# Down projections in block-product pairs, and one buffer for the sums of x and of h, in a decoder layer

## The chip, the cores and the metric

One core of a Trainium2 chip runs the whole layer in one launch. The time is device microseconds, the median of the runs of one kernel. The profile is one execution of the same program, taken by the hardware profiler; its span runs from the first to the last instruction of the program.

## What is computed

One decoder layer on x of 256 tokens by 2048 columns, float32, in four residual steps: a SwiGLU half-step, a mixer (attention beside gated linear attention), cross-attention into 256 memory tokens, and a second SwiGLU half-step. The change is in the half-steps:

```python
def swiglu(h, w_gate, w_up, w_down):
    return (jax.nn.silu(h @ w_gate) * (h @ w_up)) @ w_down

x = x + 0.5 * swiglu(rms_norm(x, ffn1_norm[l]), ffn1_w_gate[l], ffn1_w_up[l], ffn1_w_down[l])
...
x = x + 0.5 * swiglu(rms_norm(x, ffn2_norm[l]), ffn2_w_gate[l], ffn2_w_up[l], ffn2_w_down[l])
```

The gate and up weights are 2048 x 5632, the down weights 5632 x 2048.

## The kernel before

**Numbers and tiles.** Every float32 operand is split into a high and a low half (ScalarE casts the high one, L136; VectorE subtracts for the low one, L137), and a product of two operands is three matmuls: high by high, high by low, low by high. A weight block is 512 rows by 512 columns: 1 MiB, one DMA from SP (L132), one cast, one subtraction, and then for both halves of the tokens (128 each) 4 x 3 matmuls of 128x512. So a block costs TensorE 24 matmuls in plain form (`mm3`, L158 to L165).

**A half-step** (`ffn`, L345 to L397). The 5632 middle columns are 11 chunks of 512, taken in three parts: chunks 0 to 3, 4 to 7, and 8 to 10. For each chunk of a part the gate and the up projection are made, silu and the product give h, TensorE transposes it two steps later (`turn`, L349 to L357; the low half is made at L274, without high priority), and at the end of the part the down projection adds its share to x: for each of 4 output chunks, one block for each chunk of the part (L392 to L393), and an eviction to x by VectorE (L395). After the last part the first half-step starts the norm of each finished chunk (`norm_chunk`), the second one stores it.

**Seven block products.** From the second chunk on, gate and up of one chunk are made as a pair (`strassen`, L198 to L252). The left and right weights of the first two row groups and the two token halves form a 2 by 2 by 2 block product, done with seven products instead of eight. A product is 12 matmuls (`product`, L188 to L196). It wants sums of blocks: those of x are made once for each half-step (`sums_of`, L173 to L186, called at L390) and stay in the tiles sh and sl. Those of the weights are made on the way, two on VectorE (L212) and two by a DMA of POOL that adds into its target (L216). The results meet in four accumulators: c0l and x on the left, c0r and c1r on the right. The other two row groups are then added in plain form (L247 to L251). The last product, with the summed block ral, stands ahead of these groups at L245:

```python
        accumulate(ral, rbl)
        product(x, s_(2), parts(rar), False)
        ...
        product(c0r, s_(3), parts(rbr), False)
        product(x, of(b, 1), parts(ral), False)
        accs = ((c0l, x), (c0r, c1r))
```

**What sets the order.** A scheduler fixes the order of each engine's instructions ahead of the run: of those that are ready by its own account it takes the one of best priority. Weight loads, splits and sums are traced with a priority as if they stood 200 instructions earlier (`tc.high_priority(WPRI)`). On the chip each engine, and each engine's DMA queue, keeps that order. Buffers: six for raw weights, three pairs (FWB) for split weights, eight for h and for what `sums_of` needs on the way (tag "h"), one each for sh and sl.

Of the kernel before, what the change touches and what calls it, by code (L numbers as in the profile page):

```python
# [16 lines left out]
P = 128  # L17
S = 256
TT = S // P
D = 2048  # L20
NC = D // 512
# [6 lines left out]
WPRI = 200  # L28
# [17 lines left out]
PARTS = ((0, 1, 2, 3), (4, 5, 6, 7), (8, 9, 10))  # L46
# [3 lines left out]
def layer_kernel(ctx: ExitStack, tc: tile.TileContext, A: dict, out: bass.AP):  # L50
    nc = tc.nc
    V, SC, G, PE, SY = nc.vector, nc.scalar, nc.gpsimd, nc.tensor, nc.sync
# [1 line left out]
    con = ctx.enter_context(tc.tile_pool(name="con", bufs=1))  # L54
    wp = ctx.enter_context(tc.tile_pool(name="wp", bufs=3))
    sp = ctx.enter_context(tc.tile_pool(name="sp", bufs=SB))
    st = ctx.enter_context(tc.tile_pool(name="st", bufs=10))
    pa = ctx.enter_context(tc.tile_pool(name="pa", bufs=4, space=PSUM))
    pm = ctx.enter_context(tc.tile_pool(name="pm", bufs=4, space=PSUM))

# [13 lines left out]
    def FT(tag, bufs, shape, dt, name):  # L74
        return phase["pool"].tile(shape, dt, tag=tag, name=name, bufs=bufs)
# [94 lines left out]

    def sums_of(ga, gb, put):  # L173

        (ah, al), (bh, bl) = ga, gb
        fa, fb = (FT("h", 8, [P, 4, S], F32, n) for n in ("fa", "fb"))
        V.tensor_add(fa, ah.bitcast(F32), al.bitcast(F32))
        V.tensor_add(fb, bh.bitcast(F32), bl.bitcast(F32))
        t0, t1 = slice(0, P), slice(P, S)
        sa, sb = (FT("h", 8, [P, 2, 4, P], F32, n) for n in ("sa", "sb"))  # L180
        V.tensor_sub(sa[:, 0], fa[:, :, t1], fb[:, :, t1])
        V.tensor_sub(sa[:, 1], sa[:, 0], fa[:, :, t0])
        V.tensor_sub(sb[:, 0], fa[:, :, t0], fa[:, :, t1])
        V.tensor_add(sb[:, 1], fb[:, :, t0], sa[:, 1])
        for i, x in enumerate((sa, sb)):
            split(*put(i), x)  # L186

    def product(acc, lhs, w, start):  # L188

        wh, wl = w  # L190
        first = start
        for i, j, w in ((0, 0, wh), (1, 0, wh), (0, 1, wl)):
            for k in range(4):
                PE.matmul(acc, lhs(k)[i], w[:, k], start=first, stop=j == 1 and k == 3, skip_group_check=not start)  # L194
                first = False
        tick()  # L196

    def strassen(Wl, cl, Wr, cr, lhs, ab, sums, groups):  # L198

        a, b = ab  # L200
        ral, rar = load(Wl, cl, a), load(Wr, cr, a)
        rbr, rbl = load(Wr, cr, b), load(Wl, cl, b)

        def parts(src):
            with tc.high_priority(WPRI):
                wh, wl = (FT(x, FWB, [P, 4, 512], F32R, x) for x in ("wh", "wl"))
                split(wh, wl, src)
            return wh, wl

        def add(dst, x, y):  # L210
            with tc.high_priority(WPRI):
                V.tensor_add(dst, x, y)  # L212

        def accumulate(dst, x):
            with tc.high_priority(WPRI):
                G.dma_start(dst, x, accum_op=ALU.add)  # L216

        def of(g, t):
            return lambda k: lhs(4 * g + k, t)

        def s_(i):
            return lambda k: tuple(x[:, i, k] for x in sums)
# [12 lines left out]
        add(ral, ral, rbr)  # L235
        product(x, s_(1), parts(ral), False)
        with tc.high_priority(WPRI):
            V.tensor_sub(c0r, ys, x)
        product(c0l, of(b, 0), parts(rbl), False)
        accumulate(ral, rbl)  # L240
        product(x, s_(2), parts(rar), False)
        with tc.high_priority(WPRI):
            V.tensor_sub(c1r, ys, x)
        product(c0r, s_(3), parts(rbr), False)
        product(x, of(b, 1), parts(ral), False)  # L245
        accs = ((c0l, x), (c0r, c1r))
        for i, g in enumerate(groups):  # L247
            for acc, W, c in zip(accs, (Wl, Wr), (cl, cr)):
                for h, half in enumerate(wgroup(W, c, g)):
                    mm3(acc, lhs, half, False, i == len(groups) - 1 and h == 1, seeded=True)  # L250
                    tick()  # L251
        return accs  # L252

    def proj(W, c, lhs, groups, fine=None, last=False):

        n = W.shape[-1]
        acc = [pa.tile([P, n], F32, tag="acc", name="acc") for _ in range(TT)]
        groups = list(groups)
        for i, g in enumerate(groups):
            if fine and i:  # L260
                fine(4 * i)
            if last and i == len(groups) - 1:
                both = [w for half in wgroup(W, c, g) for w in half]
                for t in range(TT):
                    mm3(acc, lhs, both, i == 0, True, (t,))
                break
# [10 lines left out]
    xT = {}  # L277
# [67 lines left out]
    def ffn(pre, r, after, fine=None, last=False):  # L345
        wg, wu, wd = (A[f"{pre}_w_{n}"] for n in ("gate", "up", "down"))
        hT = {}

        def turn(f, hs):  # L349
            hi, lo = (FT("h", 8, [P, 4, S], F32R, n) for n in ("hTh", "hTl"))  # L350
            for t in range(TT):
                tp = PM([P, 4, P], "tp")
                for j in range(4):
                    PE.transpose(tp[:, j], hs[t][:, j * P:(j + 1) * P], ident)  # L354
                sl = slice(t * P, (t + 1) * P)
                split_from_psum(hi[:, :, sl], lo[:, :, sl], tp)
# [6 lines left out]
        sums = None  # L363
        for part in PARTS:
            for f in part:
                if sums is None:
                    gate = proj(wg, f, lhs_x, range(4), fine)
                    if callable(r):
                        r = r()
                else:  # L370
                    gate, upv = strassen(wg, f, wu, f, lhs_x, (0, 1), sums, (2, 3))
                sg = []
                with tc.high_priority(WPRI):
                    for t in range(TT):
                        s = W2([P, 512], "sg")
                        SC.activation(s, gate[t], AF.Silu, scale=r[:, t:t + 1])
                        sg.append(s)
                if sums is None:
# [8 lines left out]
                if sums is None:  # L387
                    sums = tuple(FT(n, 1, [P, 4, 4, P], F32R, n) for n in ("sh", "sl"))
                    with tc.high_priority(WPRI):
                        sums_of(xT[0], xT[1], lambda i: tuple(p[:, 2 * i:2 * i + 2] for p in sums))  # L390
            end = part is PARTS[-1]
            for c in range(NC):  # L392
                acc = proj(wd, c, lhs_h, part, last=last and end and c == NC - 1)  # L393
                for t in range(TT):
                    V.scalar_tensor_tensor(xs[c][:, t], acc[t], 0.5, xs[c][:, t], op0=ALU.mult, op1=ALU.add)  # L395
                if end:
                    after(c)  # L397


    def head_scale(acc, r, r2, t, scale_in, sign, name):  # L400
# [633 lines left out]
```

## Time and profile before

| | |
|---|---|
| median of 3 runs | 1975.95 us (1974.84 to 1976.38) |
| the profiled execution | 1974.94 us |
| its span | 1972.9 us |
| TensorE busy | 1942.4 us, 8760 matmuls |
| VectorE busy | 1276.1 us |
| ScalarE busy | 989.3 us |
| DMA | 416.14 MB, mean 211 GB/s |

The busy time of TensorE is modelled from matmuls that overlap, so it says that TensorE has work, not that it is at its peak. What a matmul costs is read from the distance between starts in a stretch in which it never waits. The first half-step runs from the start to about 740 us, the middle of the layer to about 1240 us, the second half-step to the end. In each half-step three stretches of down projection follow the parts. Names in the rows: acc, x and y are accumulators, xTh, hTh, sh and xTl, hTl, sl the high and low halves of x, of h and of the sums, wh and wl those of weights, raw a weight block as it was loaded.

### The profile page before, as it was taken

How to read it: one execution, taken by the hardware profiler on the slowest of the kernel's cores; microseconds unless marked ns; L12 is line 12 of the kernel's file. 1: busy time of each engine (PE TensorE's matmuls, PEld its weight loads, DVE VectorE, ACT ScalarE, POOL GpSimd, SP SyncE). 2: the span in 40 equal slices, each digit the busy share in tenths (PEclk: the TensorE clock that was granted, in tenths of full speed). 3: DMA queues.
4: the chain of work that ended last, by engine and by line, in shares of the span. 5: the costliest groups of instructions: out<-in, count | busy, mean ns of one | idle time of the engine just before them, and what ended most of it. 6: DMA issues, size and time to landing. Idle time of an engine off the chain costs nothing.

```text
span 1972.9 us, 21472 instructions
## 1 busy us (share of the span) xinstructions
PE 1942.4 (98%) x8760; PEld 1587.5 (80%) x8760; DVE 1276.1 (65%) x1027; ACT 989.3 (50%) x956; POOL 97.6 (5%) x101
## 2 busy tenths in 40 slices
PE   8999999999999999999999999899999999999999
PEld 7878887778877888778888889677788777887787
DVE  6776467774577655546785566677746777457763
ACT  5555345553355446444676445555534555335542
POOL 2000000000000000002220000000000000000000
PEclk9999999999999999999999999899999999999999
DMA  9677557775567725445466554566755777556771
GB/s 364 234 232 252 187 156 269 263 260 193 171 221 230 274 88 181 156 167 189 170 219 217 182 192 155 208 234 224 246 191 152 268 263 263 197 179 213 234 278 64
DMA packets 63294, 416.14 MB, mean 211 GB/s; under 512 B 7099, under 2 KB 8251, under 8 KB 14428
## 3 DMA queue, kind: packets, MB, share of 16 engines
q1 hardware_dynamic: 56284, 370.74, 49.7%
q0 software_dynamic: 5760, 41.95, 10.4%
q10 hardware_dynamic: 1152, 2.10, 0.3%
q8 instruction: 68, 1.11, 0.2%
q14 instruction: 30, 0.25, 0.0%
HBM read 370.72 MB, written 2.10 MB: 189 GB/s over the span
## 4 chain that ended last, share of the span: by engine, by line
PE 89%; DVE 6%; ACT 2%; issue 2%; DMA 1%; SPq 0%; POOL 0%; DVEq 0%; ACTq 0%
PE acc L164 22%; PE acc L165 22%; PE acc L163 22%; PE x L194 8%; DVE wl L137 5%; PE acc L194 4%; ACT wh L136 2%; PE y L194 2%; PE x L164 2%; PE x L165 2%; PE x L163 2%; PE tp L354 1%; DVE raw L212 1%; DMA xr<-in_xT_dram 1%; PE tp L314 0%
## 5 line engine op out<-in xcount | busy, mean ns | idle before, releaser
L137 DVE TENSOR_TENSOR wl<-raw,wh 128x2048 fp32r<-128x2048 f32 (+2 forms) x487 | 933.6, 1933 | 594.5 <-ACT wh L136 593.2
L136 ACT CAST wh<-raw 128x2048 fp32r<-128x2048 f32 (+2 forms) x487 | 777.3, 1615 | 705.0 <-PE acc L165 494.4
L164 PE MATMUL acc<-wl,xTh 128*128 128x512 f32 x1024 | 406.3, 397 | 13.7 <-DVE wl L137 13.4
L163 PE MATMUL acc<-wh,xTh 128*128 128x512 f32 x1024 | 405.9, 398 | 6.7 <-ACT wh L136 6.7
L165 PE MATMUL acc<-wh,xTl 128*128 128x512 f32 x1024 | 403.6, 394 | 0.0
L163 PE MATMUL acc<-wh,hTh 128*128 128x512 f32 x704 | 274.7, 390 | 0.0
L165 PE MATMUL acc<-wh,hTl 128*128 128x512 f32 x704 | 274.0, 389 | 0.0
L164 PE MATMUL acc<-wl,hTh 128*128 128x512 f32 x704 | 274.0, 389 | 0.0
L164 PEld LDWEIGHTS acc<-wl,xTh 128*128 128x128 f32 x1024 | 194.1, 190 | 65.3 <-DVE wl L137 24.1
L163 PEld LDWEIGHTS acc<-wh,xTh 128*128 128x128 f32 x1024 | 193.7, 190 | 50.5 <-ACT wh L136 7.6
L165 PEld LDWEIGHTS acc<-wh,xTl 128*128 128x128 f32 x1024 | 194.0, 189 | 42.3
L165 PEld LDWEIGHTS acc<-wh,hTl 128*128 128x128 f32 x704 | 132.2, 188 | 27.5
L163 PEld LDWEIGHTS acc<-wh,hTh 128*128 128x128 f32 x704 | 132.2, 188 | 27.3
L164 PEld LDWEIGHTS acc<-wl,hTh 128*128 128x128 f32 x704 | 132.2, 188 | 27.1
L216 POOL DMA_DIRECT2D raw<-raw x40 | 34.7, 867 | 1191.1 <-DVE raw L212 978.4
L212 DVE TENSOR_TENSOR raw<-raw 128x2048 f32<-128x2048 f32 x40 | 91.5, 2287 | 0.7
L163 PE MATMUL x<-wh,xTh 128*128 128x512 f32 x160 | 62.8, 392 | 0.0
L164 PE MATMUL x<-wl,xTh 128*128 128x512 f32 x160 | 62.6, 391 | 0.0
L165 PE MATMUL x<-wh,xTl 128*128 128x512 f32 x160 | 62.5, 391 | 0.0
L228 ACT COPY acc<-x 128x512 f32<-128x512 f32 x20 | 11.4, 571 | 97.9 <-PE x L194 97.9
L395 DVE SCALAR_TENSOR_TENSOR x<-acc,x 128x512 f32<-128x512 f32 x48 | 33.0, 688 | 31.7 <-PE acc L165 31.7
L163 PE MATMUL acc<-wh,mTh 128*128 128x512 f32 x128 | 50.2, 392 | 0.0
(302 smaller groups left out, 1966.0 us busy)
## 6 DMA issues: line engine op xcount, KB each, us to landing
raw<-in_ffn_w_up_dram SPq DMA_DIRECT2D x88, 1024.0 KB, 7.0
raw<-in_ffn_w_down_dram SPq DMA_DIRECT2D x88, 1024.0 KB, 5.1
raw<-in_ffn_w_gate_dram SPq DMA_DIRECT2D x85, 1024.0 KB, 7.6
raw<-in_w_in_dram SPq DMA_DIRECT2D x48, 1024.0 KB, 4.8
raw<-raw POOLq DMA_DIRECT2D x40, 1024.0 KB, 6.9
raw<-in_w_out_dram SPq DMA_DIRECT2D x16, 1024.0 KB, 4.8
raw<-in_xattn_w_k_dram SPq DMA_DIRECT2D x4, 1024.0 KB, 4.8
raw<-in_xattn_w_q_dram SPq DMA_DIRECT2D x4, 1024.0 KB, 4.7
```

Of the source, the lines that this page charges most:

```text
L136: SC.copy(wh, src)
L137: V.tensor_sub(wl, src, wh.bitcast(F32))
L163: PE.matmul(acc[t], lh, wh, start=first and i == 0, stop=False, skip_group_check=seeded)
L164: PE.matmul(acc[t], lh, wl, start=False, stop=False, skip_group_check=seeded)
L165: PE.matmul(acc[t], ll, wh, start=False, stop=last and i == len(half) - 1, skip_group_check=seeded)
L194: PE.matmul(acc, lhs(k)[i], w[:, k], start=first, stop=j == 1 and k == 3, skip_group_check=not start)
L212: V.tensor_add(dst, x, y)
L216: G.dma_start(dst, x, accum_op=ALU.add)
L228: SC.copy(c0l, x)
L354: PE.transpose(tp[:, j], hs[t][:, j * P:(j + 1) * P], ident)
L395: V.scalar_tensor_tensor(xs[c][:, t], acc[t], 0.5, xs[c][:, t], op0=ALU.mult, op1=ALU.add)
```

## The change

1. `strassen` is also used for the down projections: output chunks 0 and 1, then 2 and 3, as left and right, with the first two chunks of the part as row groups of the block product and the rest (two, or one in the last part) in plain form.
2. The sums of h that this wants are made in the last gate/up pair of each part (`mid`), in the buffer that held the sums of x. So the sums of x are written to DRAM once in each half-step, and read back after the last down pair's last product with sums, except in the last part. The DMAs are POOL's.
3. The last of the seven products moves behind the first plain group of the left weights, in all pairs.
4. `sums_of` works in place in two buffers instead of four; the layout of sh and sl follows x and h. The pool of small tiles gets 16 buffers instead of 10.

The diff, cut:

```diff
-    def sums_of(ga, gb, put):
+    def new_sums():
+        return tuple(FT(n, 1, [P, 2, 4, S], F32R, n) for n in ("sh", "sl"))
+
+    def sums_of(ga, gb):
+        t0, t1 = slice(0, P), slice(P, S)
+        sums = new_sums()
         fa, fb = (FT("h", 8, [P, 4, S], F32, n) for n in ("fa", "fb"))
...
+        for f, (h, l) in ((fa, ga), (fb, gb)):
+            V.tensor_add(f, h.bitcast(F32), l.bitcast(F32))
+        V.tensor_sub(fb[:, :, t1], fa[:, :, t1], fb[:, :, t1])
+        V.tensor_sub(fa[:, :, t1], fa[:, :, t0], fa[:, :, t1])
+        V.tensor_sub(fa[:, :, t0], fb[:, :, t1], fa[:, :, t0])
+        V.tensor_add(fb[:, :, t0], fb[:, :, t0], fa[:, :, t0])
+        for i, f in enumerate((fa, fb)):
+            split(*(x[:, i] for x in sums), f)
+        return sums
...
-    def strassen(Wl, cl, Wr, cr, lhs, ab, sums, groups):
+    def strassen(Wl, cl, Wr, cr, lhs, ab, sums, groups, mid=None, last=False):
...
         product(c0r, s_(3), parts(rbr), False)
-        product(x, of(b, 1), parts(ral), False)
+        if mid:
+            mid()
         accs = ((c0l, x), (c0r, c1r))
         for i, g in enumerate(groups):
-            for acc, W, c in zip(accs, (Wl, Wr), (cl, cr)):
+            end = i == len(groups) - 1
+            for j, (acc, W, c) in enumerate(zip(accs, (Wl, Wr), (cl, cr))):
+                if last and end and j:
...
                 for h, half in enumerate(wgroup(W, c, g)):
...
                     tick()
+                if i == j == 0:
+                    product(x, of(b, 1), parts(ral), False)
...
+            def sums_h():
+                with tc.high_priority(WPRI):
+                    hsums.append(sums_of(hT[part[0]], hT[part[1]]))
+
+            def sums_back():
+                with tc.high_priority(WPRI):
+                    hsums.append(new_sums())
+                    for x, d in zip(hsums[-1], kept):
+                        G.dma_start(x.bitcast(F32), d)
...
-                    gate, upv = strassen(wg, f, wu, f, lhs_x, (0, 1), sums, (2, 3))
+                    gate, upv = strassen(wg, f, wu, f, lhs_x, (0, 1), sums, (2, 3),
+                                         mid=sums_h if f == part[-1] else None)
...
+                        sums = sums_of(xT[0], xT[1])
+                    kept = [tc.dram_tile([P, 2, 4, S], F32, name=f"{pre}_{n}") for n in ("sh", "sl")]
+                    for x, d in zip(sums, kept):
+                        G.dma_start(d, x.bitcast(F32))
-            for c in range(NC):
-                acc = proj(wd, c, lhs_h, part, last=last and end and c == NC - 1)
-                for t in range(TT):
-                    V.scalar_tensor_tensor(xs[c][:, t], acc[t], 0.5, xs[c][:, t], op0=ALU.mult, op1=ALU.add)
-                if end:
-                    after(c)
+            for c in range(0, NC, 2):
+                accs = strassen(wd, c, wd, c + 1, lhs_h, part[:2], hsums[0], part[2:],
+                                mid=sums_back if c and not end else None, last=last and end and c == NC - 2)
+                for d, acc in zip((c, c + 1), accs):
+                    for t in range(TT):
+                        V.scalar_tensor_tensor(xs[d][:, t], acc[t], 0.5, xs[d][:, t], op0=ALU.mult, op1=ALU.add)
+                    if end:
+                        after(d)
+            sums = hsums[-1]
```

## Rows read from the trace of the kernel before

**Rows 1.** The page: busy time, share of the span and instructions of each engine; the granted clock of TensorE in 40 slices of the span, in tenths.

```profile
PE 1942.4 (98%) x8760; PEld 1587.5 (80%) x8760; DVE 1276.1 (65%) x1027; ACT 989.3 (50%) x956; POOL 97.6 (5%) x101
...
PEclk9999999999999999999999999899999999999999
```

**Rows 2.** The page: the chain that ended last, by engine and by line.

```profile
PE 89%; DVE 6%; ACT 2%; issue 2%; DMA 1%; SPq 0%; POOL 0%; DVEq 0%; ACTq 0%
PE acc L164 22%; PE acc L165 22%; PE acc L163 22%; PE x L194 8%; DVE wl L137 5%; PE acc L194 4%; ACT wh L136 2%; PE y L194 2%; PE x L164 2%; PE x L165 2%; PE x L163 2%; PE tp L354 1%; DVE raw L212 1%; DMA xr<-in_xT_dram 1%; PE tp L314 0%
```

**Rows 3.** Busy time by stretches: a stretch of plain down projection (two output chunks), and one gate/up pair. Columns: from and to, length, then busy time and instructions of PE, PEld, DVE, ACT and POOL, granted clock, share of the DMA engines, GB/s. An instruction that lies across an end of the stretch is counted.

```profile
471.70:515.20 43.50, 43.50 (x194) 36.02 (x193) 20.90 (x13) 15.28 (x8) 0.00 (x0) 1.00 0.56 193
...
323.00:366.35 43.35, 42.61 (x189) 34.42 (x188) 32.96 (x20) 23.86 (x17) 1.72 (x2) 1.00 0.71 243
```

**Rows 4.** The chain in order of time, in the gate/up pair that starts at 320.20: start, length, what.

```profile
320.20 2.75 PE x L194 x12
322.95 2.73 PE y L194 x12
...
334.80 2.72 PE acc L194 x12
337.52 1.85 PE x L194 x8
...
339.43 2.30 DVE wl L137
...
341.76 0.50 PE acc L164
342.26 0.23 PE acc L165
```

**Rows 5.** The page's costliest groups: one of the three lines of down matmuls (L164 and L165 have as many).

```profile
L163 PE MATMUL acc<-wh,hTh 128*128 128x512 f32 x704 | 274.7, 390 | 0.0
```

**Rows 6.** The timeline of the same pair: the DMA that adds into ral, the last subtraction of the block products, ScalarE's cast that waits for that DMA, and the low half of h, made in two pieces.

```profile
328.26 0.86 POOL L216 DMA_DIRECT2D raw<-raw  x1 [11.06 <-DVE wl L137]
...
335.08 0.69 DVE L243 TENSOR_TENSOR acc<-ys,x 128x512 f32<-128x512 f32 x1
...
335.28 5.51 ACT L136 CAST wh<-raw 128x2048 fp32r<-128x2048 f32 x3 [2.77 <-DMA raw<-raw]
...
343.83 0.68 DVE L274 TENSOR_TENSOR hTl<-tp,hTh 128x512 fp32r<-128x512 f32 x1
...
346.79 0.68 DVE L274 TENSOR_TENSOR hTl<-tp,hTh 128x512 fp32r<-128x512 f32 x1
```

**Rows 7.** VectorE by line in one gate/up pair (322.99 to 366.35): count, busy us, mean ns of one, idle before and what ended it. The window holds parts of three sums of weights; a pair makes two.

```profile
L137 DVE TENSOR_TENSOR wl<-raw,wh 128x2048 fp32r<-128x2048 f32 x11 | 24.8, 2289 | 10.4 <-ACT wh L136 10.3
L212 DVE TENSOR_TENSOR raw<-raw 128x2048 f32<-128x2048 f32 x3 | 6.9, 2286 | 0.0
...
L274 DVE TENSOR_TENSOR hTl<-tp,hTh 128x512 fp32r<-128x512 f32 x2 | 1.4, 682 | 0.0
L238 DVE TENSOR_TENSOR acc<-ys,x 128x512 f32<-128x512 f32 x1 | 0.7, 690 | 0.0
```

**Rows 8.** ScalarE by line in the same stretch.

```profile
L136 ACT CAST wh<-raw 128x2048 fp32r<-128x2048 f32 x11 | 20.6, 1907 | 11.4 <-PE acc L165 3.6 <-DMA raw<-raw 2.8 <-PE x L165 2.6
...
L234 ACT COPY ys<-y 128x512 f32<-128x512 f32 x1 | 0.6, 582 | 0.0
L228 ACT COPY acc<-x 128x512 f32<-128x512 f32 x1 | 0.6, 570 | 5.2 <-PE x L194 5.2
```

**Rows 9.** VectorE by line in down projections: two lines of the stretch 471.70 to 515.20, and two of the stretch 700.77 to 735.15, where the norm of finished chunks is made too.

```profile
L137 DVE TENSOR_TENSOR wl<-raw,wh 128x2048 fp32r<-128x2048 f32 x9 | 20.6, 2292 | 24.6 <-ACT wh L136 24.6
L395 DVE SCALAR_TENSOR_TENSOR x<-acc,x 128x512 f32<-128x512 f32 x4 | 2.8, 688 | 1.2 <-PE acc L165 1.2
...
L320 DVE TENSOR_TENSOR xTl<-xg,xTh 128x512 fp32r<-128x512 f32 x4 | 2.6, 688 | 0.2
L316 DVE TENSOR_TENSOR xg<-tp,gain 128x512 f32<-128x512 f32 x4 | 2.6, 682 | 0.0
```

**Rows 10.** The timeline at the start of the second half-step: TensorE, then VectorE.

```profile
1243.68 1.22 PE L163 MATMUL acc<-wh,xTh 128*128 128x512 f32 x2 [3.29 <-ACT wh L136]
1248.24 0.79 PE L164 MATMUL acc<-wl,xTh 128*128 128x512 f32 x1 [3.34 <-DVE wl L137]
...
1239.30 1.22 DVE L177 TENSOR_TENSOR fa<-xTh,xTl 128x1024 f32<-128x1024 f32 x1
...
1245.31 0.68 DVE L184 TENSOR_TENSOR sb<-fb,sa 128x512 f32<-128x512 f32 x1
1245.91 6.68 DVE L137 TENSOR_TENSOR wl<-raw,wh 128x2048 fp32r<-128x2048 f32 x3
...
1254.25 1.22 DVE L137 TENSOR_TENSOR sl<-sb,sh 128x1024 fp32r<-128x1024 f32 x1
```

**Rows 11.** The page: DMA queues with packets, MB, and the time of their packets as a share of 16 engines' span. The first holds SP's loads, the second POOL's accumulations.

```profile
q1 hardware_dynamic: 56284, 370.74, 49.7%
q0 software_dynamic: 5760, 41.95, 10.4%
```

**Rows 12.** Busy time by stretches, columns as in rows 3: after the idle time at the start of the second half-step.

```profile
1248.30:1252.90 4.60, 4.60 (x11) 3.63 (x12) 4.60 (x3) 1.34 (x2) 0.00 (x0) 0.52 0.78 289
```

More of the change, by code (lines that the diff above doesn't have):

```diff
@@ L56, in layer_kernel @@
     sp = ctx.enter_context(tc.tile_pool(name="sp", bufs=SB))
-    st = ctx.enter_context(tc.tile_pool(name="st", bufs=10))
+    st = ctx.enter_context(tc.tile_pool(name="st", bufs=16))
     pa = ctx.enter_context(tc.tile_pool(name="pa", bufs=4, space=PSUM))
@@ L165, in mm3 @@
                 PE.matmul(acc[t], ll, wh, start=False, stop=last and i == len(half) - 1, skip_group_check=seeded)
-    def sums_of(ga, gb, put):
-        (ah, al), (bh, bl) = ga, gb
-        fa, fb = (FT("h", 8, [P, 4, S], F32, n) for n in ("fa", "fb"))
[L177 to L186, printed above, removed]
+    def new_sums():
[3 more added lines that the diff above has]
+        sums = new_sums()
+        fa, fb = (FT("h", 8, [P, 4, S], F32, n) for n in ("fa", "fb"))
+        for f, (h, l) in ((fa, ga), (fb, gb)):
[7 more added lines that the diff above has]
+        return sums
     def product(acc, lhs, w, start):
@@ L221, in s_ @@
         def s_(i):
-            return lambda k: tuple(x[:, i, k] for x in sums)
+            g, t = ((1, 1), (0, 0), (0, 1), (1, 0))[i]
+            return lambda k: tuple(x[:, g, k, t * P:(t + 1) * P] for x in sums)
         x, y = PM([P, 512], "x"), PM([P, 512], "y")
@@ L244, in strassen, with proj @@
         product(c0r, s_(3), parts(rbr), False)
-        product(x, of(b, 1), parts(ral), False)
+        if mid:
+            mid()
         accs = ((c0l, x), (c0r, c1r))
         for i, g in enumerate(groups):
-            for acc, W, c in zip(accs, (Wl, Wr), (cl, cr)):
+            end = i == len(groups) - 1
+            for j, (acc, W, c) in enumerate(zip(accs, (Wl, Wr), (cl, cr))):
+                if last and end and j:
+                    both = [w for half in wgroup(W, c, g) for w in half]
+                    for t in range(TT):
+                        mm3(acc, lhs, both, False, True, (t,), seeded=True)
+                    break
                 for h, half in enumerate(wgroup(W, c, g)):
-                    mm3(acc, lhs, half, False, i == len(groups) - 1 and h == 1, seeded=True)
+                    mm3(acc, lhs, half, False, end and h == 1, seeded=True)
                     tick()
+                if i == j == 0:
+                    product(x, of(b, 1), parts(ral), False)
         return accs
-    def proj(W, c, lhs, groups, fine=None, last=False):
+    def proj(W, c, lhs, groups, fine=None):
         n = W.shape[-1]
@@ L261, in proj @@
                 fine(4 * i)
-            if last and i == len(groups) - 1:
-                both = [w for half in wgroup(W, c, g) for w in half]
-                for t in range(TT):
-                    mm3(acc, lhs, both, i == 0, True, (t,))
-                break
             for h, half in enumerate(wgroup(W, c, g, fine if i == 0 else None)):
@@ L361, in lhs_h @@
             return tuple(p[:, k % 4, sl] for p in hT[k // 4])
-        sums = None
+        sums = kept = None
         for part in PARTS:
+            end = part is PARTS[-1]
+            hsums = []
+            def sums_h():
[6 more added lines that the diff above has]
+                        G.dma_start(x.bitcast(F32), d)
             for f in part:
-                if sums is None:
+                plain = sums is None
+                if plain:
                     gate = proj(wg, f, lhs_x, range(4), fine)
@@ L377, in ffn @@
                         sg.append(s)
-                if sums is None:
+                if plain:
                     upv = proj(wu, f, lhs_x, range(4))
@@ L386, in ffn @@
                 later(2, lambda f=f, hs=hs: turn(f, hs))
-                if sums is None:
-                    sums = tuple(FT(n, 1, [P, 4, 4, P], F32R, n) for n in ("sh", "sl"))
+                if plain:
                     with tc.high_priority(WPRI):
-                        sums_of(xT[0], xT[1], lambda i: tuple(p[:, 2 * i:2 * i + 2] for p in sums))
-            end = part is PARTS[-1]
-            for c in range(NC):
-                acc = proj(wd, c, lhs_h, part, last=last and end and c == NC - 1)
-                for t in range(TT):
-                    V.scalar_tensor_tensor(xs[c][:, t], acc[t], 0.5, xs[c][:, t], op0=ALU.mult, op1=ALU.add)
-                if end:
-                    after(c)
+                        sums = sums_of(xT[0], xT[1])
[6 more added lines that the diff above has]
+                for d, acc in zip((c, c + 1), accs):
+                    for t in range(TT):
+                        V.scalar_tensor_tensor(xs[d][:, t], acc[t], 0.5, xs[d][:, t], op0=ALU.mult, op1=ALU.add)
+                    if end:
+                        after(d)
+            sums = hsums[-1]
     def head_scale(acc, r, r2, t, scale_in, sign, name):
```

## The prediction, made before the changed kernel was run

> **What bounds the kernel now.** I read the busy line of the page first: TensorE is busy for 98% of the span, VectorE for 65%, and the granted clock stands at 9 tenths or more in nearly every slice [rows 1]. Then the chain that ended last: 89% of it is TensorE work [rows 2]. So a matmul taken away is worth its time as long as nothing else ends later in its place. Then the stretches, because the change touches two kinds. In a stretch of plain down projection TensorE never pauses, VectorE works 20.90 of 43.50 us and the DMA engines 0.56 of the time. One gate/up pair of the block-product kind takes 43.35 us, VectorE works 32.96 of it and the DMA engines 0.71 [rows 3]. Last the chain in time inside such a pair: the products follow one another until the seventh, then a wait shows [rows 4].
>
> **Part 1, the matmuls removed.** A down pair had eight block products in its first two groups, now it has seven, so 12 matmuls go. Six pairs in each half-step, twice: 144 of 2112 (three lines of 704 [rows 5]). Their price: in the plain down stretch the window touches 194, two of them across its ends, so 43.50 / 192 = 0.2266 us each [rows 3]; in block products 12 take 2.72 to 2.76 us, 0.228 each [rows 4]. Afterwards 12 x 84 = 1008 are in products and 960 in plain groups: 1008 x 0.228 + 960 x 0.2266 = 447.4 against 2112 x 0.2266 = 478.6, a gain of 31.2 us. Bounds: all at 0.2266 gives 32.6, all at 0.228 gives 29.9.
>
> The Trainium skill (TensorE: Matmul & The Clock Gate, section Back-to-back issue gap) has another price for a stream of weight loads and matmuls: about 131 ns for 512 columns. By that page the 144 would be worth an estimated 18.9 us and the forecast some 12 us later. No stretch here shows it; the rows above have 227 to 228 ns, and they decide.
>
> **Part 2, the product that moves behind the first plain group (all 32 pairs, 20 of them old).** In the pair shown the last product starts at 337.52 and the fifteenth matmul from there is over at 342.26: 4.74 us where 15 x 0.229 = 3.43 would do, so 1.3 us are lost [rows 4]. The cause: its operand is summed by a DMA that POOL issues at 328.26, ScalarE waits 2.77 us for it until 335.28, and the split on VectorE follows [rows 6]. After the change 24 matmuls (5.5 us) of the left weight block stand in between, and that block needs no sum. VectorE is through with its last subtraction at 335.77 [rows 6]; the block's split takes 2.29 us [rows 7] and ends at 338.06, where TensorE wants it at 337.75. So 0.3 us remains. The summed block, cast from 335.28, is split by 340.4, wanted at 343.0: hidden. Old pairs: 20 x (1.3 - 0.3) = 20 us gained (bounds 0 and 26). New pairs: 12 x 0.3 = 3.6 us lost (bounds 0 and 15.6).
>
> **Part 3, what a down pair adds beside TensorE.** Three more splits, two sums of weight blocks, two subtractions: 3 x 2.29 + 2 x 2.29 + 2 x 0.69 = 12.8 us on VectorE; on ScalarE three casts of 1.91 and two short copies [rows 7, 8]. In a pair of four groups VectorE had 8 x 2.29 + 4 x 0.69 = 21.1 [rows 7, 9], now 33.9 beside 180 x 0.228 = 41 of TensorE. That is the load of a gate/up pair, which hides it: nothing beyond the 0.3 above. In the last part (three groups) it is 16.5 + 12.8 = 29.3 beside 132 x 0.228 = 30.1. The cover is gone there: in the first half-step the norm of the first two chunks falls into the second pair, eight operations of 0.69, 5.5 us [rows 9], so 34.8 - 30.1 = 4.7 late. For the other three such pairs, 97% full, I take 1 us each (bounds 0 and 3, a cast and the gap behind it). Sum 7.7 us (bounds 0 and 14).
>
> **Part 4, h of the last chunk.** Its low half is made at normal priority, today 23.6 and 26.6 us after the pair's first product at 320.20 [rows 4, 6], and the plain groups that want it came late enough. In a last-part pair group 10 is the first plain group, wanted after 17.3 us. VectorE has no gap before 335.77, then two splits go ahead (to 340.35), then the two subtractions of 0.68: 341.7 against 337.5, 4.2 us, twice: 8.4 us (bounds 0, if an earlier gap takes them, and 19.6, if they stay where they are).
>
> **Part 5, the sums of h.** Six times two additions of 1.22, four operations of 0.68, two splits of 1.22: 7.6 us of VectorE [rows 10], against 43.35 - 32.96 = 10.4 us idle in such a pair [rows 3]. They must wait for the last reader of the sums of x, 17.3 us into the last gate/up pair, and are wanted 27 us later: hidden but for a late split, 0.5 us each, 3 us. Bounds 0 and the stall at the start of the second half-step, which is the slower case below. The sums of x there and in the first half-step cost what they cost today: as many operations of the same sizes.
>
> **Part 6, the DMAs.** 24 more accumulations and, per half-step, 2 MiB written and twice 2 MiB read back, all from POOL. A MiB takes 0.497 x 1972.9 / 370.74 x 1.049 = 2.8 us of all engines when loaded and 0.104 x 1972.9 / 40 = 5.1 when accumulated (40 of them, two in each of 20 pairs) [rows 11]. A four-group pair then fills 8 x 2.8 + 2 x 5.1 = 32.6 of 41 us, 38.2 with a read back; a three-group pair 27 of 30.1. POOL's queue has nothing else in these stages: a read back waits for the fourth product with sums, and the next accumulation is issued some 20 us later. SP's loads wait, as they do now, for the accumulation that frees a buffer. I take 0.5 us for each read back, 2 us; bounds 0 and 5.6 for each of the six transfers of 2 MiB, 34.
>
> **Part 7, the ends.** In the first half-step chunks 2 and 3 now finish together, so their norms both fall behind the last matmuls: 5.5 us of VectorE beside the first groups of the next stage, which want those chunks last; 1.5 us (bounds 0 and 5.5). At the end of the kernel the last eviction follows 12 matmuls of one half, as now: 0.
>
> **Sum.** -31.2 - 20 + 3.6 + 7.7 + 8.4 + 3 + 2 + 1.5 = -25.0. The profiled execution took 1974.9 (span 1972.9 and 2.0 around it), 1.0 below the median of the runs. 1974.9 - 25.0 + 1.0 = 1951 us. Its own range: 1939 to 1962 (half of the bounds of parts 2 to 4).
>
> **The rivals.**
> 1. All is hidden. Parts 3 to 7 cost nothing: -31.2 - 20 + 3.6 = -47.6, 1928 us. For it: VectorE has 10 us to spare in each old pair, and its order is made ahead of the run, so small work can go early. Against it: 29.3 of 30.1 us in the last part.
> 2. The move buys half. If ScalarE's queue still has the summed block ahead of the left block, the wait only changes its name: 10 instead of 20 gained, 7.8 instead of 3.6 lost, 14 us more: 1965 us. For it: today the cast is queued exactly so, behind the DMA [rows 6].
> 3. Loads come late. If each new pair waits 2 us for weights, 24 us more: 1975 us, no change. For it: 27 of 30.1 us. Against it: the accumulations are needed late.
> 4. Slower: the sums of h stand ahead of the next weight split on VectorE. That is what happens at the start of the second half-step: additions and subtractions from 1239.30 to 1245.99, the weights' split only then, TensorE idle for 3.29 and 3.34 us [rows 10]. And the granted clock is 0.52 from 1248.3 to 1252.9, the lower level of 1.2 GHz, after those idle times; 11 matmuls take 4.6 us there in place of 2.5 [rows 12]. Together 8.7 us, at six hand-overs 52. The 3 of part 5 goes, and 16 of parts 3 and 4, since VectorE catches up in a stall: -25 + 52 - 19 = +8, 1984 us. It decides from (25 + 19) / 6 = 7.3 us per hand-over. Against it: a hand-over has no arrears of a norm, and the left block can be split before the sums are free.
>
> **How the numbers follow.** Chances: forecast 0.55, all hidden 0.17, half 0.12, late loads 0.05, slower 0.11. The range of 1925 to 1968 holds the first three, 0.84. About 4 us (0.2%) is what a measurement can tell from no change: faster 0.84, same 0.05, slower 0.11.
>
> **What would show it.** Matmuls 8616 instead of 8760; gate/up pairs of 42.3 instead of 43.35 us with the waits behind the seventh product gone; four-group down pairs of some 41.3 us instead of 43.5; VectorE near 1276 + 12 x 12.8 + 6 x 7.6 = 1475 us. A wait of some 4 us on the low half of h in each last part, with VectorE full there. Wrong would be: TensorE idle for over 7 us at each hand-over, or in every down pair behind a load, or gate/up pairs still at 43.3.

## The result and the profile after

The changed kernel takes 1979.78 us (median of 20 runs, 1975.63 to 1983.17), the kernel before 1974.95 on the same chips. The ratio is 1.0022, 95% interval 1.0015 to 1.0029: slower by 5 us, where 24 us less had been forecast and the range ended at 1968. The profiled execution has a span of 1975.3 us, 2.4 more than before.

The page of the changed kernel, its busy lines, the granted clock, the chain, the largest groups with a wait, and the issues of the accumulations and the read back (KB each, median us to landing):

```profile
PE 1908.5 (97%) x8616; PEld 1560.5 (79%) x8616; DVE 1455.1 (74%) x1159; ACT 1075.7 (54%) x1028; POOL 125.8 (6%) x137
PEclk8999999999999999999999999999999999999999
...
PE 50%; DVE 26%; ACT 10%; issue 9%; DMA 5%; SPq 0%; ACTq 0%; POOL 0%; DVEq 0%; POOLq 0%
...
L163 PE MATMUL acc<-wh,hTh 128*128 128x512 f32 x240 | 94.4, 397 | 18.2 <-ACT wh L136 18.2
...
L197 PE MATMUL x<-wh,sh 128*128 128x512 f32 x256 | 72.0, 403 | 12.2 <-ACT wh L136 11.5
...
raw<-raw POOLq DMA_DIRECT2D x64, 1024.0 KB, 6.9
...
sl<-ffn_sl POOLq DMA_DIRECT2D x4, 1024.0 KB, 9.9
sh<-ffn_sh POOLq DMA_DIRECT2D x4, 1024.0 KB, 14.0
```

The 144 matmuls are gone and VectorE has most of the work that was forecast (1455 us; 1475 expected). But TensorE's share of the chain, the work that ended last followed back in time, fell from 89% [rows 2] to 50%: on the path stand now splits of VectorE and casts of ScalarE. The group to look at is the first: TensorE waits 18.2 us for casts ahead of the first plain group of a down pair.

Stretches of the changed kernel, a row for each pair (columns as in [rows 3]): a gate/up pair, the last gate/up pair of a part with the sums of h in it, the two down pairs of that part, the first gate/up pair after them, a pair of the last part, and 2.9 us inside that one:

```profile
318.58:360.86 42.28, 42.11 (x190) 34.47 (x189) 32.80 (x20) 23.81 (x17) 1.73 (x2) 1.00 0.72 249
403.13:445.45 42.32, 42.14 (x190) 34.46 (x188) 38.40 (x28) 25.69 (x19) 1.74 (x2) 1.00 0.66 236
445.45:490.63 45.18, 42.62 (x190) 34.49 (x188) 34.92 (x21) 22.43 (x16) 1.74 (x2) 1.00 0.73 241
490.63:534.23 43.60, 41.41 (x182) 33.51 (x180) 32.57 (x20) 21.44 (x13) 2.87 (x4) 1.00 0.82 289
534.23:577.27 43.04, 41.39 (x182) 33.51 (x180) 31.98 (x18) 22.84 (x15) 1.74 (x2) 1.00 0.74 248
661.83:700.53 38.70, 34.15 (x141) 26.60 (x140) 29.12 (x19) 18.29 (x18) 0.87 (x1) 0.96 0.67 217
687.30:690.20 2.90, 2.90 (x8) 2.22 (x7) 0.04 (x1) 0.00 (x0) 0.00 (x0) 0.50 0.99 418
```

A gate/up pair takes 42.3 us, as forecast, against 43.35 [rows 3]; the sums of h cost it nothing, though VectorE is 91% busy there. The down pairs take 45.2 and 43.6 us where 41.3 was forecast and plain down projection takes 43.5 [rows 3]. The first gate/up pair behind them (43.0) is slower than it was, since before the four of them took 42.6 each, as here:

```profile
277.45:320.04 42.59, 42.06 (x182) 33.31 (x180) 31.80 (x19) 22.81 (x15) 1.71 (x2) 1.00 0.73 247
```

In the last part 38.7 us are spent on 132 matmuls worth 30.

Why a down pair waits, in the first of the two (445.45 to 490.63). Its ScalarE, the accumulation that POOL issues, its TensorE, and its VectorE (start us, us):

```profile
453.03 7.33 ACT L136 CAST wh<-raw 128x2048 fp32r<-128x2048 f32 x4
460.26 0.58 ACT L281 CAST hTh<-tp 128x512 fp32r<-128x512 f32 x1
462.21 1.91 ACT L136 CAST wh<-raw 128x2048 fp32r<-128x2048 f32 x1 [1.37 <-DMA raw<-raw]
464.02 0.58 ACT L281 CAST hTh<-tp 128x512 fp32r<-128x512 f32 x1
464.50 1.90 ACT L136 CAST wh<-raw 128x2048 fp32r<-128x2048 f32 x1
```

```profile
455.27 0.87 POOL L219 DMA_DIRECT2D raw<-raw  x1 [10.38 <-DVE wl L137]
```

```profile
464.24 0.39 PE L163 MATMUL acc<-wh,hTh 128*128 128x512 f32 x1
464.47 0.39 PE L163 MATMUL x<-wh,hTh 128*128 128x512 f32 x1
466.45 0.50 PE L163 MATMUL acc<-wh,hTh 128*128 128x512 f32 x1 [1.60 <-ACT wh L136]
466.79 0.39 PE L164 MATMUL acc<-wl,hTh 128*128 128x512 f32 x1
```

```profile
457.79 4.49 DVE L137 TENSOR_TENSOR wl<-raw,wh 128x2048 fp32r<-128x2048 f32 x2
462.19 0.69 DVE L247 TENSOR_TENSOR acc<-ys,x 128x512 f32<-128x512 f32 x1
462.79 6.69 DVE L137 TENSOR_TENSOR wl<-raw,wh 128x2048 fp32r<-128x2048 f32 x3
```

The third plain matmul does not belong to the left block: it starts at 466.45, just when the cast begun at 464.50 is over, and the left block was cast long before, as the last of the four that end at 460.36. The order of instructions, fixed ahead of the run, has in such a pair (buffer numbers of the second down pair of the first part; blocks 1710/1711 left, 1738 summed, 1756 right):

```
ScalarE   CAST wh_1710<-raw_1708
          CAST wh_1738<-raw_1586   waits for the accumulating DMA
          CAST wh_1756<-raw_1754
TensorE   acc_1596<-wh_1710   x_1594<-wh_1710
          acc_1597<-wh_1756   acc_1598<-wh_1756
          acc_1596<-wl_1711   ...
```

Two matmuls of the right block stand ahead of the left block's first low half. The cast of the right block is queued on ScalarE behind that of the summed block, which starts when the accumulation lands: 462.21 - 455.27 = 6.94 us after its issue; in eleven of the twelve down pairs it is 6.9 to 7.6. So the 22 other matmuls of the left block, whose split is done at 462.79 + 2.29 = 465.1, wait for a sum that is needed 5 us later. TensorE is idle for 1.3 to 2.2 us at this place in eleven of the twelve down pairs, and for 1.6 to 2.2 us in the four first gate/up pairs (between the starts of two matmuls it is 0.2 us more). That is the wait of [rows 6] under a new name.

### The profile page after: what moved, and what is told of

Its sections match the earlier page's. It is cut to its first block, busy times and chain, and to the rows that moved or that the text cites. A ratio compares the mean times of both kernels' runs of the same rounds, so it can differ in the third digit from the quotient of the medians.

```text
span 1975.3 us, 21548 instructions
## 1 busy us (share of the span) xinstructions
PE 1908.5 (97%) x8616; PEld 1560.5 (79%) x8616; DVE 1455.1 (74%) x1159; ACT 1075.7 (54%) x1028; POOL 125.8 (6%) x137
## 4 chain that ended last, share of the span: by engine, by line
PE 50%; DVE 26%; ACT 10%; issue 9%; DMA 5%; SPq 0%; ACTq 0%; POOL 0%; DVEq 0%; POOLq 0%
DVE wl L137 15%; PE acc L164 13%; PE acc L165 12%; PE acc L163 12%; ACT wh L136 10%; DVE raw L215 7%; PE x L197 5%; DMA raw<-raw 2%; DMA raw<-in_ffn_w_gate_dram 2%; PE x L165 1%; PE x L164 1%; PE x L163 1%; PE acc L197 1%; DVE h L407 1%; DVE acc L242 1%
## 5 line engine op out<-in xcount | busy, mean ns | idle before, releaser
L137 DVE TENSOR_TENSOR wl<-raw,wh 128x2048 fp32r<-128x2048 f32 (+2 forms) x523 | 1009.4, 1955 | 419.1 <-ACT wh L136 418.3
L136 ACT CAST wh<-raw 128x2048 fp32r<-128x2048 f32 (+2 forms) x523 | 840.8, 1638 | 601.6 <-PE acc L165 260.8
L164 PE MATMUL acc<-wl,xTh 128*128 128x512 f32 x1024 | 402.9, 393 | 6.5 <-DVE wl L137 6.1
L165 PE MATMUL acc<-wh,xTl 128*128 128x512 f32 x1024 | 400.5, 391 | 0.0
L164 PEld LDWEIGHTS acc<-wl,xTh 128*128 128x128 f32 x1024 | 193.3, 189 | 54.6 <-DVE wl L137 15.1
L165 PEld LDWEIGHTS acc<-wh,xTl 128*128 128x128 f32 x1024 | 193.4, 189 | 39.8
L215 DVE TENSOR_TENSOR raw<-raw 128x2048 f32<-128x2048 f32 x64 | 146.2, 2285 | 0.6
L163 PE MATMUL acc<-wh,hTh 128*128 128x512 f32 x240 | 94.4, 397 | 18.2 <-ACT wh L136 18.2
L164 PE MATMUL acc<-wl,hTh 128*128 128x512 f32 x240 | 94.3, 393 | 3.7 <-DVE wl L137 3.7
L165 PE MATMUL acc<-wh,hTl 128*128 128x512 f32 x240 | 94.5, 394 | 0.2
L197 PE MATMUL x<-wh,sh 128*128 128x512 f32 x256 | 72.0, 403 | 12.2 <-ACT wh L136 11.5
L197 PE MATMUL x<-wl,sh 128*128 128x512 f32 x256 | 70.3, 396 | 0.1
L163 PEld LDWEIGHTS acc<-wh,hTh 128*128 128x128 f32 x240 | 45.1, 189 | 31.4 <-ACT wh L136 22.6
L197 PE MATMUL x<-wh,sl 128*128 128x512 f32 x256 | 68.9, 390 | 0.0
L165 PE MATMUL x<-wh,xTl 128*128 128x512 f32 x160 | 62.3, 390 | 0.0
L164 PE MATMUL x<-wl,xTh 128*128 128x512 f32 x160 | 62.3, 389 | 0.0
```

The source lines that it names most:

```text
L163: PE.matmul(acc[t], lh, wh, start=first and i == 0, stop=False, skip_group_check=seeded)
L164: PE.matmul(acc[t], lh, wl, start=False, stop=False, skip_group_check=seeded)
L165: PE.matmul(acc[t], ll, wh, start=False, stop=last and i == len(half) - 1, skip_group_check=seeded)
```

## Experiments

The theory to test (**T**): TensorE, by its order, waits for the right block's cast, which stands behind a wait for the accumulating DMA. Its rivals: VectorE is short of time in the down pairs, or late loads, the read back above all, hold TensorE. Gains and losses below are differences of medians; the intervals of the runs leave some 1.5 to 3 us to either side. Lengths of pairs come from one profiled execution each.

**The move alone, on the kernel before**

```diff
-        product(x, of(b, 1), parts(ral), False)
...
+                if i == j == 0:
+                    product(x, of(b, 1), parts(ral), False)
```

> The kernel before with part 2 of the forecast alone: the last product of each of its 20 gate/up pairs is emitted behind the left block of the first plain group; down projections plain as before. Part 2 as forecast: 20 x (1.3 - 0.3) = 20 us less, 1955 us, each pair 42.3 instead of 43.35 us. If the wait only changes its name (rival 2), 10 us less, 1965. If the move itself is what made the changed kernel slow, 1975 or more.

Measured: 1965.31 us, ratio 0.9953 (0.9938 to 0.9968), 9 us less. A gate/up pair, and a first one of a part, in this kernel:

```profile
319.13:361.51 42.38, 42.34 (x190) 34.55 (x189) 32.79 (x20) 23.79 (x17) 1.72 (x2) 1.00 0.73 248
275.12:319.13 44.01, 41.53 (x181) 33.52 (x180) 31.69 (x18) 22.74 (x15) 1.71 (x2) 1.00 0.70 239
```

Fifteen pairs gain the 1.0 us each that was forecast, one nothing. The four first pairs lose 0.5 to 1.4 each: a wait of 2.5 us for a cast ahead of the plain group appears in the second row's pair. So a wait of this kind comes with the move itself, without a down pair in the kernel.

**The right block first**

```diff
+            gens = [wgroup(W, c, g) for W, c in zip((Wl, Wr), (cl, cr))]
...
                 if i == j == 0:
+                    right = list(gens[1])
                     product(x, of(b, 1), parts(ral), False)
```

> The changed kernel, in which the right block of the first plain group is cast and split ahead of the summed block; matmuls and DMAs are the same. Theory (TensorE's order in the down pairs puts two matmuls of the right block ahead of the left block's low half, and that block's cast stands in ScalarE's queue behind a cast that waits for the accumulating DMA): the waits of 1.6 to 2.4 us on the cast of that block go from 12 down pairs and 4 first gate/up pairs, some 25 to 30 us less, about 1952 us, four-group down pairs of some 41.5 us instead of 43.0. Rival VectorE full in the down pairs: the same work on VectorE, so the same 1978 us. Rival late loads: the same 1978 us.

Measured: 1959.66 us, ratio 0.9927 (0.9912 to 0.9942), 20 us less than the changed kernel, with its matmuls, DMAs and work on VectorE. Pairs of this kernel: gate/up, the two down pairs, the first gate/up pair after them:

```profile
314.34:356.14 41.80, 41.80 (x190) 34.46 (x188) 32.79 (x20) 23.83 (x17) 1.72 (x2) 1.00 0.73 252
439.78:483.17 43.39, 42.42 (x189) 34.49 (x188) 34.91 (x21) 22.53 (x16) 1.74 (x2) 1.00 0.75 251
483.17:524.78 41.61, 41.47 (x182) 33.51 (x180) 30.99 (x19) 21.24 (x13) 2.87 (x4) 1.00 0.80 291
524.78:569.39 44.61, 42.73 (x181) 34.88 (x180) 33.73 (x18) 23.37 (x16) 1.74 (x2) 0.96 0.76 250
```

T holds for the down pairs of four groups: 45.2 and 43.6 become 43.4 and 41.6, 13.5 us over the eight of them. Sixteen gate/up pairs give another 7 us, as the wait of 0.4 us for the left block's split goes too. In the first gate/up pairs the wait on the right block goes, but TensorE now waits 1.7 to 2.5 us ahead of the third product, and nothing is gained. Nor is it in the last parts, where other waits take its place. From the start of the last part to the end the second half-step takes 79.6 us instead of 78.0; two waits of TensorE in it, and a stretch right behind the second:

```profile
1900.08 0.73 PE L164 MATMUL acc<-wl,hTh 128*128 128x512 f32 x2 [1.47 <-DVE wl L137]
1902.88 0.80 PE L165 MATMUL acc<-wh,hTl 128*128 128x512 f32 x1 [2.07 <-DVE hTl L286]
...
1903.20:1907.20 4.00, 4.00 (x10) 3.14 (x10) 0.22 (x1) 0.00 (x0) 0.00 (x0) 0.50 1.01 426
```

A split and the low half of h hold TensorE here, and the granted clock is 0.50 behind them, its lower level of 1.2 GHz.

**The sum on VectorE instead of the DMA, in down pairs**

```diff
-        accumulate(ral, rbl)
+        if Wl is Wr:
+            add(ral, ral, rbl)
+        else:
+            accumulate(ral, rbl)
```

> The changed kernel, in which the last sum of weight blocks of each of the 12 down pairs is an addition of 2.29 us on VectorE instead of the accumulating DMA; gate/up pairs as they are. Theory of the wait for the accumulating DMA: that wait goes in the 12 down pairs (1.6 to 2.4 us each), and 2.29 us of VectorE come in: about 20 us less in the eight four-group pairs and the four last-part pairs together where VectorE has room, nothing in the last part: 1962 us. Rival VectorE full: 12 x 2.3 = 27 us more, 2006 us. Rival late loads: 12 accumulations of 5.1 us of all engines fewer, so earlier loads, 1970 us.

Measured: 1984.51 us, ratio 1.0047 (1.0030 to 1.0064), 5 us more than the changed kernel. T's 1962 us was missed, and so were the rivals' 2006 and 1970. The waits of TensorE in a four-group down pair of this kernel:

```profile
PE acc L197 <- DVE wl L137: 1.0, 1, 1.0
PE acc L163 <- ACT wh L136: 0.6, 1, 0.6
```

Before the plain group 0.6 us are left of the 2.2 in the same pair, but the addition pushes the split ahead of it back, 1.0 us. VectorE is 79% busy in that pair, and still has not 2.3 us to give at this place; in the last part the wait for a split grows from 1.9 to 3.7 us. The share of a pair does not tell whether a moment has room.

**The old place in down pairs**

```diff
+        if Wl is Wr:
+            product(x, of(b, 1), parts(ral), False)
...
-                if i == j == 0:
+                if i == j == 0 and Wl is not Wr:
```

> The changed kernel with the last product moved in the gate/up pairs alone; in the 12 down pairs it stands ahead of the plain groups, as all had it before. Part 2 of the forecast prices the old place at 1.3 us per pair and the new at 0.3: by that 12 us more, 1991. By the trace of the changed kernel the new place costs 1.7 to 2.4 us in down pairs; if the old costs 1.3, 6 us less, 1973 us.

Measured: 1970.12 us, ratio 0.9972 (0.9961 to 0.9983), 10 us less. In the pair that took 43.60 us the old place gives 43.19, in the second pair of the first part 42.55 instead of 43.01. Over the eight pairs of four groups it is 5.3 us. So there the move, as it was made, cost 0.7 us each, where 1.0 less had been forecast.

**No read back**

```diff
-                    kept = [tc.dram_tile([P, 2, 4, S], F32, name=f"{pre}_{n}") for n in ("sh", "sl")]
...
-                                mid=sums_back if c and not end else None, last=last and end and c == NC - 2)
+                                last=last and end and c == NC - 2)
```

> The changed kernel without the sums of x written out and read back (12 MiB of transfers); left out is the return to the sums of x, the later gate/up pairs take the sums of h in their place. Theory of ScalarE's queue and TensorE's order: the waits of 1.7 to 2.4 us on the cast of the right block stay in all 12 down pairs and 4 first gate/up pairs; only the waits of 0.6 to 1.5 us ahead of the third product of the first gate/up pairs go, 4 us less, 1975 us. Rival late loads: the transfers crowd the weight loads everywhere behind them, 20 us less, 1960 us.

Measured: 1978.00 us, ratio 1.0013 (1.0004 to 1.0022). Against 1.0022 (1.0015 to 1.0029) the difference is not settled; 20 us from the read back are out. The wait on the right block stays, 1.7 us in a first gate/up pair, and hides most of what the read back delays, as the last experiment below shows.

**Plain down projections in the last part**

```diff
-                                         mid=sums_h if f == part[-1] else None)
+                                         mid=sums_h if f == part[-1] and not end else None)
...
+            if end:
+                for c in range(NC):
+                    acc = proj(wd, c, lhs_h, part, last=last and c == NC - 1)
```

> The changed kernel with plain down projections in the last part of each half-step (4 pairs, 48 matmuls more, and no sums of h there). The matmuls cost 48 x 0.2285 = 11 us; by the trace of the changed kernel its last parts lose 7.7 and 7.4 us at h of the last chunk, about 6.3 us in the second pair of the first half-step, 3.1 and 1.8 us in those of the second. If these waits belong to the pairs, 26 - 11 = 15 us less, 1964 us. If they only move (norm and h late in any case), 11 us more, 1990.

Measured: 1964.01 us, ratio 0.9946 (0.9931 to 0.9961), 16 us less with 48 matmuls more. The waits belong to the pairs: seven products in a part of three groups save 11 us and cost 16 + 11 = 27.

**h of the very last chunk first**

```diff
+                with tc.high_priority(WPRI if f == PARTS[-1][-1] else 0):
                     split_from_psum(hi[:, :, sl], lo[:, :, sl], tp)
```

> The changed kernel, in which the split of h of the very last chunk of a half-step has the priority of the weights' splits; the same instructions. Part 4 of the forecast (the two subtractions stand behind two weight splits): the wait of 2.0 + 0.4 us and the stretch at the lower granted clock behind it go, twice, 6 to 8 us less, 1973 us. Rival: the last part's pairs are held by VectorE's sum of work, so the wait moves to a weight split and the time stays at 1979 us.

Measured: 1971.11 us, ratio 0.9979 (0.9970 to 0.9989), 9 us less. VectorE in the last part of the changed kernel, the wait of TensorE there, and that pair with h first:

```profile
679.46 6.69 DVE L137 TENSOR_TENSOR wl<-raw,wh 128x2048 fp32r<-128x2048 f32 x3
686.06 1.28 DVE L282 TENSOR_TENSOR hTl<-tp,hTh 128x512 fp32r<-128x512 f32 x2
691.89 0.69 DVE L421 SCALAR_TENSOR_TENSOR x<-acc,x 128x512 f32<-128x512 f32 x1 [4.55 <-PE acc L165]
```

```profile
686.20 0.50 PE L164 MATMUL acc<-wl,hTh 128*128 128x512 f32 x1 [1.86 <-DVE wl L137]
```

```profile
661.61:695.80 34.19, 31.93 (x142) 25.27 (x140) 27.92 (x18) 18.28 (x17) 0.87 (x1) 1.00 0.75 245
```

The two subtractions for the low half of h stand behind three splits, and behind them VectorE has nothing to do for 4.55 us: an order, not a lack of time. What TensorE waits for at 686.20 is the third of these splits; the low half of h holds it for 0.4 us more. Of the 4.5 us that the pair gains, 2.0 and 0.4 are these two waits and 0.4 a part of the wait for the right block. The other 1.7 are the granted clock: in the changed kernel it is 0.50 from 687.3 to 690.2, behind the waits (the lower level, 1.2 GHz), and over the whole pair here it is 1.00.

**Plain down projections, with the move and the right block first**

> The kernel before with the last product moved and the right block cast first; all down projections plain. From the pairs of the kernels that ran: 16 gate/up pairs of 41.82 instead of 43.34 us and 4 first pairs of 41.6 instead of 42.6, so 28 us less, 1946 us. Then the down pairs as such are worth only 1946 - 1941 = 5 us in c13_both, though its 96 matmuls fewer are worth 21. Rival: the wait for the sum is still there in the first pairs, which have no h to transpose, 1.5 us each: 1952 us.

The edit is that of the first two experiments on the kernel before. Measured: 1950.50 us, ratio 0.9872 (0.9858 to 0.9887), between both. The first pairs have 41.6 us as T has it; the others keep 42.0 to 42.1 for the most part. So the 25 us that had been forecast for the whole change are to be had without a down pair.

**Both edits**

> The changed kernel with both edits: the right block of the first plain group cast ahead of the summed block, and plain down projections in the last parts. If the two act on different waits, the gains of 20 and 16 us add, less the waits on the right block in the last parts, some 6 us, which both take away: 1950 us. If they act on the same waits, 1960 us.

Measured: 1941.37 us, ratio 0.9832 (0.9817 to 0.9846). The gains add fully (20 + 16 gives 1944). The 6 us taken off for an overlap were wrong, since the right block first had gained nothing in the last parts. Against the kernel with plain down projections it is 9 us for 96 matmuls fewer, and 2.7 of the 9 lie in the middle of the layer (shown in the next section), not in the down pairs.

**The sums computed again, in place of the read back**

```diff
-                    hsums.append(new_sums())
-                    for x, d in zip(hsums[-1], kept):
-                        G.dma_start(x.bitcast(F32), d)
+                    hsums.append(sums_of(xT[0], xT[1], raw=True))
```

> As c13_both, and the sums of x are computed again on VectorE in the second down pair (7.6 us of VectorE each, four times) instead of written out and read back (12 MiB of DMA). If the read back makes the weights late, the waits ahead of the third product of the first gate/up pairs (1.9 to 2.7 us in the kernel with the right block first) go: 8 to 10 us less than c13_both, 1940 us. If VectorE is what is short there, 4 to 8 us more than c13_both, 1956 us.

Measured: 1959.44 us, ratio 0.9923 (0.9908 to 0.9937), 18 us more. The second down pair of a part and the first gate/up pair after it:

```profile
1444.63:1498.21 53.58, 45.24 (x182) 35.72 (x180) 35.56 (x22) 23.44 (x15) 1.72 (x2) 0.90 0.65 217
1498.21:1539.82 41.61, 41.47 (x181) 33.51 (x180) 31.96 (x18) 22.98 (x15) 1.72 (x2) 1.00 0.75 256
```

The first gate/up pairs lose their wait (41.6 us), which shows that the read back holds them. But the intermediate values of the sums take one of the buffers of the weight loads, and TensorE waits 7.2 us at a stretch for a cast in this down pair. The two like it in the first half-step take 44.3 and 44.5 us instead of 41.6. This changes two things, VectorE's work and the buffers, so what lengthens the down pairs is not told apart.

**The read back later, in the loads' queue**

```diff
         rbr, rbl = load(Wr, cr, b), load(Wl, cl, b)
+        if callable(sums):
+            sums = sums()
...
-                        G.dma_start(x.bitcast(F32), d)
+                        SY.dma_start(x.bitcast(F32), d)
```

> As c13_both, but the sums of x are read back through the queue of the weight loads, behind the first two or three loads of the pair that wants them. If the read back made these loads late (recomputing the sums took 1.4 to 3.6 us from each of the four pairs), 8 to 9 us less than c13_both, 1932 us. If the sums themselves then come late, TensorE waits ahead of the second product of those pairs, 1945 us.

Measured: 1931.08 us, ratio 0.9774 (0.9758 to 0.9791), 10 us less than with POOL's early read back: the version to keep, 2.3% faster than before. ScalarE ahead of the first gate/up pair with the early read back, then with the late one:

```profile
517.37 1.91 ACT L136 CAST wh<-raw 128x2048 fp32r<-128x2048 f32 x1 [3.64 <-DMA raw<-in_ffn_w_gate_dram]
524.51 1.91 ACT L136 CAST wh<-raw 128x2048 fp32r<-128x2048 f32 x1 [5.23 <-DVE raw L215]
```

```profile
511.81 1.91 ACT L136 CAST wh<-raw 128x2048 fp32r<-128x2048 f32 x1 [3.98 <-PE acc L165]
518.96 1.91 ACT L136 CAST wh<-raw 128x2048 fp32r<-128x2048 f32 x1 [5.24 <-DVE raw L217]
```

With the early read back the cast waits for the gate block's load, and VectorE's sum of weight blocks and the product with it are late by that. With the late one it waits for a buffer that TensorE frees, which costs nothing; the first gate/up pairs take 41.6 us instead of 43.0 to 45.2. The transfers differ by few us: POOL issues the two 16.2 and 17.1 us into the down pair, ahead of both gate loads (from 17.9 us); SP issues them 18.2 and 22.6 us in, behind the first gate load and behind all four loads. The edit changes the queue as well as the time, and no run tells the two apart.

## Why the prediction was wrong

The sum missed by 2.4 + 25.0 = 27.4 us of the span. By stretches of the profiled executions: the eight four-group down pairs take 354.7 us together where 8 x 41.3 and the transposes of h in four of them (0.9 each) make 334: 21 over. The four first gate/up pairs take 175.8 instead of 170.4 before, and 166.4 was forecast: 9 over. The last parts are 16 us worse than plain ones, forecast 7.8 (-11 + 7.7 + 8.4 + 1.5 + 4 x 0.3): 8 over. Parts 5 and 6 had 5 us for what lies in these stretches. About 6 us came back elsewhere. Of these 2.7 lie in the middle of the layer, which no part of the sum speaks of; the stretch of the same TensorE instructions, before and after:

```profile
744.97:1239.36 494.39, 494.39 (x2401) 411.09 (x2400) 299.00 (x424) 274.35 (x430) 47.90 (x43) 1.00 0.51 181
747.17:1238.90 491.73, 491.73 (x2401) 410.87 (x2400) 300.37 (x428) 275.71 (x432) 48.13 (x43) 1.00 0.51 182
```

Kernels made from the changed one have 491.7 there, the two made from the one before 494.4. The likely reason, not run by itself, is the 16 buffers for small tiles, which this code uses. Another 1.7 lie at the start of the second half-step, where the granted clock is 0.50 for 6.7 us instead of 10.1.

- **Part 1** held in its count, 8616 matmuls. Their price is measured only together with the waits. The Trainium skill (TensorE: Matmul & The Clock Gate, section Back-to-back issue gap) has some 131 ns for a matmul of 512 columns in a stream of weight loads and matmuls. The trace does not agree: the gate/up pair of 41.80 us has 180 of them, 0.227 us each when the 0.9 us of its transposes are taken off.
- **Part 2, old pairs** held in 15 of 20 (42.3 us, -1.05 each); the four first pairs of a part got 0.4 to 2.3 us longer instead.
- **Part 2, new pairs, is the step that failed.** "That block needs no sum" is true of the left block, and the 0.3 us was worked out for it alone. I asked whether its operands were ready, not in which order TensorE takes the blocks, nor what is queued on ScalarE behind the wait for the DMA: the right block's cast, wanted after two matmuls. TensorE is idle for 1.3 to 2.2 us by it in 11 of 12 down pairs, 18.2 us together, where 3.6 had been forecast, and in the 4 first gate/up pairs; the bound of 15.6 (1.3 each) was taken from the old wait and was too low. The experiment with the right block first shows the cause in the down pairs of four groups: with the same work it gives back 13.5 of their 21 us.
- **Rival 2** had the mechanism, "the wait only changes its name", with the wrong block ahead of which it falls, so its price was too small. **Rival 4** ended near the measured time by luck: a hand-over costs some 1.2 us (0.9 + 0.3, in the first down pair of a part with the right block first), not 8.7.
- **Part 3** was right that VectorE has time over a pair of four groups, but the sum on VectorE shows that there is none at that place. Its 7.7 us for the last part cannot be told apart from parts 2 and 4 in the 27 us that the pairs cost there.
- **Part 4** held in kind: low halves of h behind weight splits. Its size came out by luck: 8.4 us forecast, 8.7 gained when h goes first, but the two waits are 2.4 us in a pair, not 4.2, and most of that is ahead of a weight split; 1.7 us are the lower clock behind them, which the sum does not have.
- **Part 5** held in the gate/up pairs: 42.32 us at 91% of VectorE. **Part 7** was not measured by itself.
- **Part 6** was low. At 0.5 us per read back it looks confirmed by the experiment without it, where the other wait covers it; once that is gone, it is 10 us in four places, 2.5 each.

## What to carry to other kernels

When a wait is to be hidden behind other work, follow all that is queued behind the waiting instruction on its own engine, and read the order in which the consumer takes the blocks: what is ready by its data can still stand behind the wait. Price a removed wait with the next one in its place; here three lay on top of one another (cast, read back, h), and each showed its full worth only when the one above it was gone. A product saved is worth its matmuls only where its preparation is hidden: in parts of three groups it was not, as ordered here. The right block first and h first were not tried together there, so whether an order exists that hides it stays open.

## What the runs showed of the hardware

An accumulating DMA of 1 MiB between two buffers lands 6.9 us after its issue (median of 64), in stages whose DMA engines are 0.7 to 0.8 busy, so it is a latency to plan for. And 2 MiB read back on POOL's queue, 2 to 6 us earlier than on SP's, hold a cast for 3.64 us, in pairs whose DMA engines are busy for 0.8 of the time. After idle times of 1.3 and 1.86 us, 3 us apart, TensorE's granted clock was 0.50 for some 3 us, which cost 1.7 us on top of the waits.
